# A gated linear attention and differential attention decoder on one core: runs of alternating half-array products, a bias table read from shifted copies, fewer zero products, another order in the router

## The chip, the cores and the metric

The kernel runs on one core of one Trainium2 chip. Its time is the device time of one execution in microseconds (us). The engines of the core work from queues of their own: TensorE (PE, with its weight loads PEld), VectorE (DVE), ScalarE (ACT), GpSimd (POOL) and SyncE (SP), which here issues nearly all transfers.

## What is computed

Two layers over 256 tokens of 1024 features, batch 1, all in float32. Layer 0 mixes the tokens with gated linear attention (four heads, a state of 128 x 256 for each, carried over four chunks of 64 tokens), layer 1 with differential attention (eight heads, two score maps of 64 features each, a bias from a table of relative positions). After each mixer stand a layer norm, a mixture of 16 experts with a hierarchical router (best group of four, then the two best experts in it), and another layer norm.

```python
def step(state, inp):                       # gated linear attention, per chunk of 64 tokens
    q_c, k_c, v_c, dec = inp
    state = dec[..., None] * state + jnp.einsum('bhck,bhcv->bhkv', k_c, v_c)
    o = jnp.einsum('bhck,bhkv->bhcv', q_c, state)
    return state, o

bias = rel_table[rel_bucket(kpos[None, :] - qpos[:, None])].transpose(2, 0, 1)
def probs(qb, kk):                          # differential attention
    s = jnp.einsum('bhqd,bhkd->bhqk', qb, kk) * scale + bias
    return jax.nn.softmax(jnp.where(visible, s, NEG_INF), axis=-1)
w = probs(q1b, k1) - lam * probs(q2b, k2)

for e in range(16):                         # mixture of experts
    hdn = jax.nn.silu(t @ w_gate[e]) * (t @ w_up[e])
    y = y + combine[:, e:e + 1] * (hdn @ w_down[e])
```

## The kernel before

**Order.** The code is written as a list of operations on tiles; a planner orders each engine's queue from it by the order of the text, by modelled costs and by when buffers are free, and `tc.issue_after(x)` puts an operation behind x in the queue of its engine. So operations of later lines can stand ahead of earlier ones that still wait, as long as no such rule forbids it.

**Weights.** SP loads all weights into a ring of 16 slots of 1 MB (`ring_slot`, L246; `load_cols`, L249; `load_moe`, L266) and three spare tiles x0 to x2 (`spare_tile`, L290). A slot is filled again when its last reader is done. The first 16 tiles of the first mixture go into the ring while the first mixer runs; `late_loads` (L338) queues the others, the table for the attention's bias and the weights of layer 1.

**The recurrence** (`head_proj`, L926; `head_scan`, L957). For each of four heads a projection of 8 steps runs on TensorE, with the weights split in two halves by ACT (L118) and DVE (L119). `head_scan` then goes chunk pair by chunk pair: two products k^T v (L964), which read the upper and the lower 64 rows and write two PSUM banks (`pB`, of which there are two), then for each of the two chunks a DVE step that decays the state and adds the product (L969, L971), and a product with the queries (L973), which writes the upper or lower half of the output partitions. The scan of one head is written after the projection of the next.

**The bias table.** `constants` (L358) makes a table of 8 heads x 384 positions and writes it to DRAM (`tvd`, L387, on POOL's queue). `late_loads` reads it back as T1 with each partition one element further on (L342). Partition p needs the window that starts at 127 - p, so T1 is upside down; `flip` (L1018) turns it with four products with a reversal matrix (L1023) and four ACT copies (L1024) into T, and POOL writes the mask (L1025). `moe` calls it as `side` behind expert 9 of the first mixture (L808).

**The router** (`out_norm`, L424; `norm_rstd`, L223; the head of `moe`, L464). The logits are taken from the tokens before the layer norm, gathered in `pl`, copied by DVE (L448) and folded by a product (L452); the mean and the reciprocal deviation then correct them (L457, L460). DVE compares them (L490 to L499), TensorE counts positions (L503, L504) and DVE makes one-hot matrices (L516). Meanwhile ACT applies the layer norm to the tokens in four pieces (L479), with the bias `nr` of L475, and splits them (L529); the gather products (L548) need both.

**The mixtures.** For each expert: 16 products with gate and up weights (L604), 8 with the down weights (L632), transposes (L589, L620) and a scatter (L664). The last one is `down_last` (L644).

**Between the mixtures' end and the attention** TensorE runs 25 zero products (`zero`, L179, its record is L181; called at L818) while DVE and ACT do the second layer norm (L837 to L843). Then `transposes` (L167) turns the tokens, with nine more zero products (`filler=9`, L1046) between the first and the second block of tokens of its first pair, and `affine_T` (L1034) scales and splits the result on ACT and DVE.

**The scores** (L1058). For each pair of heads, for each head, for each block of 128 queries: two products of 64 rows (L1071), one for each map, into one bank; DVE adds the bias and takes the minimum (L1073), ACT the exponential (L1076).

Of the kernel before, what the change touches and what calls it, by code (L numbers as in the profile page):

```python
# [10 lines left out]
F32 = mybir.dt.float32  # L11
# [32 lines left out]
def body(ctx, tc, x, w_in, wa_out, kv_w, wq, wb_out, wg, wu, wd, gate2, rows, rtab, lng, lnb, cblob, pblob, onehot, out):  # L44
# [25 lines left out]
    def sm(shape, tag, dt=F32, bufs=2):  # L70
        return small.tile(shape, dt, tag=tag, bufs=bufs, name=nm(tag))
# [150 lines left out]

    def norm_rstd(st, nd):  # L223
        a = sm([128, 2], "lna")
        dve.tensor_mul(a, nd, nd)
        dve.tensor_scalar(a, a, -EPS, None, op0=ALU.add)
        v = sm([128, 2], "lnv")
        for b in range(2):
            dve.tensor_scalar(v[:, b:b + 1], st[1][:, b, 0:1], st[1][:, b, 1:2], 1.0 / D, op0=ALU.add, op1=ALU.mult)
        dve.tensor_sub(v, v, a)  # L230
        y = sm([128, 2], "lny")
        act.activation(y, v, AF.Abs_reciprocal_sqrt)
        newton(y, v, a)
        return y

# [54 lines left out]
    def spare_tile(i, shape, dt, name):  # L290
        return spare.tile(shape, dt, tag=f"x{i}", bufs=1, name=name)
# [42 lines left out]
    next(moe_loads)  # L334
    tvd = dram.tile([8, 384], F32, name="tvd")
    late = {}

    def late_loads():  # L338
        moe_loads.send([spare_tile(j, [128, 2048], F32, nm("W")) for j in (2, 0, 1)])
        T1 = spare_tile(1, [128, 8, 256], F32, "T1")  # L340
        tap = tvd[:]
        sp.dma_start(T1, bass.AP(tensor=tap.tensor, offset=tap.offset, ap=[[1, 128], [384, 8], [1, 256]]))  # L342
        next(moe_loads)
        late["T1"] = T1
        late["v"] = [load_cols([(kv_w, 1024, 512)])]
        late["p"] = [load_cols([(wq[0], h * 128, 128), (wq[0], 512 + h * 128, 128), (kv_w, h * 128, 128), (kv_w, 512 + h * 128, 128)]) for h in range(4)]
        late["v"].append(load_cols([(kv_w, 1536, 512)]))
        late["o"] = [load_cols([(wb_out[0], j * 512, 512)]) for j in range(2)]
        late["m"] = load_moe(1, M1)
        next(late["m"])  # L350
# [7 lines left out]
    def constants():  # L358
# [27 lines left out]
        dve.tensor_scalar(tv, p[0:8, 0:384], -1.0, None, op0=ALU.mult)  # L386
        pool.dma_start(tvd, tv)  # L387

        lp = scr[0:1, 1792:1920].rearrange("p (q f) -> p q f", q=2)
# [34 lines left out]
    def out_norm(mp, layer, slots, xs, scale, xtf):  # L424
# [22 lines left out]
        lt = mp.tile([128, S], F32, tag="hi", bufs=3, name=nm("lt"))  # L447
        dve.tensor_copy(lt, pl[:, 0:256])  # L448
        rstd = norm_rstd(st, nd)
        pl = pB()  # L450
# [7 lines left out]
        for b in range(2):  # L458
            bs = slice(b * 20, b * 20 + 20)
            dve.scalar_tensor_tensor(lgf[:, bs], lgf[:, bs], rstd[:, b:b + 1], rowb[layer][:, 1], op0=ALU.mult, op1=ALU.add)  # L460
        return lg, rstd, nd, fold


    def moe(layer, M, lg, rstd, nd, fold, side=None):  # L464
        with tc.tile_pool(name=f"moe{layer}", bufs=1) as mp:
# [7 lines left out]

            nr = sm([128, 2], "nr")
            dve.tensor_mul(nr, nd, rstd)  # L475
            for h in range(2):
# [339 lines left out]
            if layer == 0:  # L816
                p = pB()
                for i in range(25):  # L818
                    zero(p)
# [106 lines left out]
    def head_proj(h, side=iter(())):  # L926
# [28 lines left out]
        return qT, kd, v  # L955

    def head_scan(h, qT, kd, v):  # L957
        st = None
        po = pC()
        for b in range(2):  # L960
            pk = [pB(), pB()]
            for cc in range(2):
                rs = slice(cc * 64, cc * 64 + 64)
                pe.matmul(pk[cc][:, 0:256], kd[rs, b], v[rs, b], start=True, stop=True)  # L964
            for cc in range(2):
                c = 2 * b + cc
                ns = scr[:, c % 3 * 256:c % 3 * 256 + 256]
                if c == 0:
                    dve.tensor_copy(ns, pk[cc][:, 0:256])  # L969
                else:  # L970
                    dve.scalar_tensor_tensor(ns, st, dec[:, h, c:c + 1], pk[cc][:, 0:256], op0=ALU.mult, op1=ALU.add)  # L971
                st = ns
                pe.matmul(po[cc * 64:cc * 64 + 64, b * 256:b * 256 + 256], qT[:, c * 64:c * 64 + 64], ns, start=True, stop=True)  # L973
        act.activation(o_sb[:, :, h * 256:h * 256 + 256], po.rearrange("p (b d) -> p b d", b=2), AF.Copy)
# [42 lines left out]

    def flip():  # L1018
        T1 = late["T1"]
        late["T"] = T = spare_tile(0, [128, 8, 256], F32, "T")  # L1020
        for q in range(4):
            p = pC()
            pe.matmul(p, cb[:, C_AN:C_AN + 128], T1[:, 2 * q:2 * q + 2].rearrange("p h j -> p (h j)"), start=True, stop=True)  # L1023
            act.activation(T[:, 2 * q:2 * q + 2].rearrange("p h j -> p (h j)"), p, AF.Copy)  # L1024
        pool.memset(T[0:64, :, 192:256], 1e30)  # L1025

    moe(0, M0, *rt_, flip)


    with tc.tile_pool(name="mix1", bufs=1) as mp:  # L1030
# [3 lines left out]
        def affine_T(kp, p):  # L1034
# [10 lines left out]
            dve.tensor_sub(xlo[:, 2 * kp:2 * kp + 2], f, xhi[:, 2 * kp:2 * kp + 2])  # L1045
        transposes(xa, affine_T, filler=9)  # L1046
        xs = lambda k: (xhi[:, k], xlo[:, k])
# [10 lines left out]
        def scores(hp, qk):  # L1058

            res = []  # L1060
            for hh in range(2):
                h = 2 * hp + hh
                rs = slice(hh * 64, hh * 64 + 64)
                wt_ = wx[:, h % 4]
                for b in range(2):
                    n = 128 * (b + 1)
                    p = pB()
                    sc = mp.tile([128, 2, 256], F32, tag="sc", bufs=2, name=nm("sc"))
                    m_ = sm([128, 2], "mrow", bufs=4)
                    for w in range(2):  # L1070
                        pe.matmul(p[:, w * 256:w * 256 + n], qk[rs, w, b * 128:b * 128 + 128], qk[rs, 2 + w, 0:n], start=True, stop=True)  # L1071
                    for w in range(2):
                        dve.tensor_tensor_reduce(out=sc[:, w, 0:n], in0=p[:, w * 256:w * 256 + n], in1=T[:, h, 256 - n:256], scale=1.0, scalar=3e38,  # L1073
                                                 op0=ALU.add, op1=ALU.min, accum_out=m_[:, w:w + 1])
                    for w in range(2):
                        act.activation(sc[:, w, 0:n], sc[:, w, 0:n], AF.Exp, scale=-1.0, bias=m_[:, w:w + 1], accum_out=es[:, b, h, w:w + 1])  # L1076
# [5 lines left out]
                res.append(wt_)  # L1082
            return res

# [124 lines left out]
```

## Time and profile before

| | before |
|---|---|
| median of 3 runs | 780.58 us (780.30 to 781.99) |
| the profiled execution | 782.23 us, of which the span is 780.6 us |
| PE, PEld | 751.2 us (96%), 404.2 us (52%) |
| DVE, ACT, POOL | 362.7 us (46%), 299.7 us (38%), 8.4 us (1%) |
| HBM | 244.19 MB read, 1.06 MB written, 315 GB/s in the mean |
| mean granted TensorE clock | 0.991 |

The span is the time from the first to the last instruction of the program; the rest of the time lies around it. Matmuls are pipelined and their ends are modelled, so a busy PE says that the matmul queue has work, not how much of the array is used. A float32 product appears as two records. An engine name with q is its sequencer; "issue" is time in which an engine waited for nothing that the profile shows. In a row, "out<-in" names the tiles that are written and read.

### The profile page before, as it was taken

The page shows a single profiled execution, that of the slowest core. Times are in us where ns is not written, and L with a number is a line of the kernel's source. Part 1 is how long each engine was busy: PE and PEld are TensorE (multiplying, and loading weights), DVE is VectorE, ACT ScalarE, POOL GpSimd, SP SyncE. Part 2 cuts the span into 40 slices and gives each one's busy share as a digit, 9 for nine tenths or more (in the row PEclk, how much of TensorE's full clock was granted, in tenths as well). Part 3 has the DMA queues.
Part 4 walks back from the last instruction along what each step waited for, and adds up shares of the span by engine and source line. Part 5 has one row for each costly group of instructions (what it writes and reads, how often), then busy time and mean ns, then how long its engine had stood idle before and what let it go on. Part 6 is the DMA issues. An engine that isn't in the chain of part 4 may idle for free. (4 is left out here: it accounts for less than half of the span.)

```text
span 780.6 us, 10650 instructions
## 1 busy us (share of the span) xinstructions
PE 751.2 (96%) x3762; PEld 404.2 (52%) x3762; DVE 362.7 (46%) x959; ACT 299.7 (38%) x655; POOL 8.4 (1%) x20
## 2 busy tenths in 40 slices
PE   7999999999999999999899999999999999999993
PEld 5887677534333433433689887763343243343331
DVE  3645576533363422422567777773344432332225
ACT  4444466523222331312557666562132232242123
POOL 1100000000000000000000000000000000000000
PEclk9999999999999999999999999999999999999997
DMA  7999448499999999999998336619999999999941
GB/s 217 312 385 392 168 164 295 152 381 397 394 386 393 392 395 396 393 392 367 290 363 314 144 111 215 216 56 370 393 395 395 394 391 390 397 394 392 391 168 56
DMA packets 131792, 246.02 MB, mean 315 GB/s; under 512 B 7916, under 2 KB 38101, under 8 KB 131734
## 3 DMA queue, kind: packets, MB, share of 16 engines
q1 hardware_dynamic: 131270, 244.68, 86.3%
q8 instruction: 32, 0.52, 0.3%
q10 hardware_dynamic: 432, 0.59, 0.2%
q14 instruction: 26, 0.21, 0.1%
q0 software_dynamic: 32, 0.01, 0.0%
HBM read 244.19 MB, written 1.06 MB: 314 GB/s over the span
## 5 line engine op out<-in xcount | busy, mean ns | idle before, releaser
L604 PE MATMUL pB<-W,xg 128*64 128x512 f32 x1056 | 258.7, 602 | 0.0
L604 PEld LDWEIGHTS pB<-W,xg 128*64 128x64 f32 x1056 | 69.1, 136 | 117.1 <-issue 110.2
L632 PE MATMUL pC<-W,ht 128*64 128x512 f32 x248 | 112.9, 594 | 0.0
L632 PE MATMUL pB<-W,ht 128*64 128x512 f32 x248 | 112.9, 594 | 0.0
L640 ACT ACTIVATE o<-pB,wst 64x512 fp32r<-64x512 f32 x31 | 21.1, 682 | 221.8 <-PE pC L632 208.4
L591 DVE TENSOR_SCALAR st<-pC 128x256 fp32r<-128x256 f32 x33 | 14.0, 425 | 155.2 <-PE pC L589 155.2
L119 DVE TENSOR_TENSOR lo<-W,hi 128x512 fp32r<-128x512 f32 x96 | 66.3, 696 | 39.9 <-PE pA L128 26.4
L118 ACT ACTIVATE hi<-W 128x512 fp32r<-128x512 f32 x96 | 59.5, 630 | 51.4 <-PE pA L129 29.8
L632 PEld LDWEIGHTS pB<-W,ht 128*64 128x64 f32 x248 | 33.3, 137 | 62.8 <-issue 61.2
L664 PE MATMUL pA<-o,st 128*128 128x512 f32 x132 | 40.2, 423 | 2.7 <-DVE o L658 2.1
L623 DVE COPY ht<-pC 128x256 f32<-128x256 f32 x33 | 14.0, 424 | 60.8 <-PE pC L620 60.7
L613 DVE TENSOR_TENSOR hd<-sl,pB 128x256 f32<-128x256 f32 x33 | 13.9, 422 | 56.7 <-ACT sl L611 56.6
L548 PE MATMUL pC<-OH,xs 128*128 128x256 f32 (+1 forms) x256 | 36.4, 292 | 3.1 <-ACT xg L555 1.9
L664 PEld LDWEIGHTS pA<-o,st 128*128 128x128 f32 x132 | 21.9, 188 | 33.5 <-issue 23.5
L548 PEld LDWEIGHTS pC<-OH,xs 128*128 128x128 f32 x256 | 32.8, 190 | 10.9 <-ACT xs L529 6.1
L127 PE MATMUL pA<-x1Thi,hi 128*128 128x256 f32 x128 | 36.5, 288 | 0.0
L632 PEld LDWEIGHTS pC<-W,ht 128*64 128x64 f32 x248 | 33.3, 137 | 6.1 <-issue 5.1
L128 PE MATMUL pA<-x1Tlo,hi 128*128 128x256 f32 x128 | 36.2, 285 | 0.0
L129 PE MATMUL pA<-x1Thi,lo 128*128 128x256 f32 x128 | 35.6, 288 | 0.0
L611 ACT ACTIVATE sl<-pB 128x256 f32<-128x256 f32 x33 | 12.7, 385 | 58.6 <-PE pB L604 58.4
L128 PE MATMUL pA<-lo,xThi 128*128 128x384 f32 (+1 forms) x96 | 35.0, 364 | 0.0
L129 PE MATMUL pA<-hi,xTlo 128*128 128x384 f32 (+1 forms) x96 | 34.7, 361 | 0.0
(340 smaller groups left out, 1148.1 us busy)
## 6 DMA issues: line engine op xcount, KB each, us to landing
W<-in_moe_w_gate_dram SPq DMA_DIRECT2D x132, 512.0 KB, 10.9
W<-in_moe_w_up_dram SPq DMA_DIRECT2D x132, 512.0 KB, 10.8
W<-in_moe_w_down_dram SPq DMA_DIRECT2D x66, 1024.0 KB, 12.0
W<-in_a_w_in_dram SPq DMA_DIRECT2D x16, 256.0 KB, 6.3
W<-in_a_w_in_dram SPq DMA_DIRECT2D x4, 1024.0 KB, 13.3
W<-in_a_w_out_dram SPq DMA_DIRECT2D x4, 1024.0 KB, 14.9
W<-in_kv_w_dram SPq DMA_DIRECT2D x4, 1024.0 KB, 8.9
W<-in_b_w_q_dram SPq DMA_DIRECT2D x16, 256.0 KB, 5.4
```

The source lines that it names most:

```text
L118: act.activation(hi, src, AF.Copy)
L119: dve.tensor_sub(lo, src, hi)
L127: pe.matmul(o, l[0], r[0], start=first, stop=False, skip_group_check=skip)
L128: pe.matmul(o, l[0], r[1], start=False, stop=False, skip_group_check=skip)
L129: pe.matmul(o, l[1], r[0], start=False, stop=last, skip_group_check=skip)
L548: pe.matmul(o, xs[k][:, q // 2, q % 2], OH[g][:, q % 2].rearrange("p e s -> p (e s)"), start=q == 0, stop=q == 3)
L591: dve.tensor_scalar(st, p[0:2 * m, 0:256], 0.0, None, op0=ALU.is_gt)
L604: mm = pe.matmul(p[c * m:c * m + m, 0:2 * fw].rearrange("p (g f) -> p g f", g=2), xg(k), w[:, :, kk, c * fw:c * fw + fw], start=k == 0, st ...
L623: dve.tensor_copy(ht, pt[:, 0:n * 128].rearrange("p (c t) -> p c t", c=n))
L632: mm = pe.matmul(p[2 * c // nt][c * m:c * m + m, 0:w], ht[:, q % n, (q // n) * m:(q // n) * m + m], wd_[q // 2][:, q % 2, c * w:c * w + w] ...
L640: act.activation(hi, src, AF.Copy, scale=ws[a:a + m, 0:1])
L664: pe.matmul(y[b][c], st[:, b * 128:b * 128 + 128], o[c], start=False, stop=last, skip_group_check=True)
```

## The change

Four parts. (1) `head_scan` issues the four products k^T v of a head as one run, with the lower and the upper rows in turn, then the four DVE steps with a place of its own for each state, then the four products with the queries as one run, from the last chunk to the first. `scores` takes the block of queries as the outer loop and issues the four products of both heads as one run, again in turn. `together` chains the products of a run by `issue_after`. (2) The table is written 128 times, one copy for each partition, to a second DRAM tile by a further transfer on POOL's queue; T is read from it directly, each partition from its own copy and one element earlier than the one before; the reversal products and the copies go, the mask stays. T takes x0 at the load, T1's x1 is not used. (3) 23 zero products in place of 25 after the first mixture, none in place of nine in the transposes. (4) `nr` is made in `norm_rstd`, and the copy of the logits is put behind it.

```diff
-    def norm_rstd(st, nd):
+    def norm_rstd(st, nd, nr):
         a = sm([128, 2], "lna")
...
         newton(y, v, a)
-        return y
+        return y, dve.tensor_mul(nr, nd, y)
...
+    tve = dram.tile([128, 8, 384], F32, name="tve")
...
-        T1 = spare_tile(1, [128, 8, 256], F32, "T1")
-        tap = tvd[:]
-        sp.dma_start(T1, bass.AP(tensor=tap.tensor, offset=tap.offset, ap=[[1, 128], [384, 8], [1, 256]]))
+        T = spare_tile(0, [128, 8, 256], F32, "T")
+        tap = tve[:]
+        sp.dma_start(T, bass.AP(tensor=tap.tensor, offset=tap.offset + 127, ap=[[8 * 384 - 1, 128], [384, 8], [1, 256]]))
         next(moe_loads)
...
         pool.dma_start(tvd, tv)
+        pool.dma_start(tve, tvd[:].unsqueeze(0).broadcast_to([128, 8, 384]))
...
-        dve.tensor_copy(lt, pl[:, 0:256])
-        rstd = norm_rstd(st, nd)
+        nr = sm([128, 2], "nr")
+        rstd, root = norm_rstd(st, nd, nr)
+        with tc.issue_after(getattr(root, "ins", root)):
+            dve.tensor_copy(lt, pl[:, 0:256])
...
-            nr = sm([128, 2], "nr")
-            dve.tensor_mul(nr, nd, rstd)
...
-                for i in range(25):
+                for i in range(23):
                     zero(p)
...
+    def together(mms):
+        prev = None
+        for mm in mms:
+            with tc.issue_after(prev) if prev else contextlib.nullcontext():
+                prev = mm()
+                prev = getattr(prev, "ins", prev)
+
     def head_scan(h, qT, kd, v):
-        st = None
+        pk = [pB(), pB()]
+        half = lambda cc: slice(cc * 64, cc * 64 + 64)
+        col = lambda b: slice(b * 256, b * 256 + 256)
+        together([lambda b=b, cc=cc: pe.matmul(pk[cc][:, col(b)], kd[half(cc), b], v[half(cc), b], start=True, stop=True) for b in range(2) for cc in (1, 0)])
+        st = []
+        for c in range(4):
+            ns, p = scr[:, c * 256:c * 256 + 256], pk[c % 2][:, col(c // 2)]
+            if c == 0:
+                dve.tensor_copy(ns, p)
+            else:
+                dve.scalar_tensor_tensor(ns, st[-1], dec[:, h, c:c + 1], p, op0=ALU.mult, op1=ALU.add)
+            st.append(ns)
         po = pC()
-        for b in range(2):
-            pk = [pB(), pB()]
-            for cc in range(2):
-                rs = slice(cc * 64, cc * 64 + 64)
-                pe.matmul(pk[cc][:, 0:256], kd[rs, b], v[rs, b], start=True, stop=True)
-            for cc in range(2):
...
-                pe.matmul(po[cc * 64:cc * 64 + 64, b * 256:b * 256 + 256], qT[:, c * 64:c * 64 + 64], ns, start=True, stop=True)
+        together([lambda c=c: pe.matmul(po[half(c % 2), col(c // 2)], qT[:, c * 64:c * 64 + 64], st[c], start=True, stop=True) for c in (3, 2, 1, 0)])
...
-    def flip():
...
-    moe(0, M0, *rt_, flip)
+    def mask():
+        pool.memset(late["T"][0:64, :, 192:256], 1e30)
+
+    moe(0, M0, *rt_, mask)
...
-        transposes(xa, affine_T, filler=9)
+        transposes(xa, affine_T)
...
         def scores(hp, qk):
-            for hh in range(2):
-                h = 2 * hp + hh
-                for b in range(2):
-                    n = 128 * (b + 1)
-                    p = pB()
...
-                    for w in range(2):
-                        pe.matmul(p[:, w * 256:w * 256 + n], qk[rs, w, b * 128:b * 128 + 128], qk[rs, 2 + w, 0:n], start=True, stop=True)
+            hs = (2 * hp, 2 * hp + 1)
+            for b in range(2):
+                n = 128 * (b + 1)
+                ps = [pB(), pB()]
+                rows_ = lambda hh: slice(hh * 64, hh * 64 + 64)
+                together([lambda w=w, hh=hh: pe.matmul(ps[hh][:, w * 256:w * 256 + n], qk[rows_(hh), w, b * 128:b * 128 + 128], qk[rows_(hh), 2 + w, 0:n], start=True, stop=True)
+                          for w in range(2) for hh in (1, 0)])
+                for h, p in zip(hs, ps):
```

## Rows read from the trace of the kernel before

**Rows 1.** Stages: length; PE, PEld, DVE, ACT, POOL busy (xcount); clock; DMA share; GB/s.
```profile
30.00:92.00 62.00, 61.85 (x316) 47.58 (x315) 31.53 (x65) 27.58 (x60) 1.43 (x2) 0.97 0.93 327
...
149.00:365.00 216.00, 214.53 (x966) 80.18 (x964) 74.16 (x176) 55.17 (x119) 0.52 (x1) 1.00 1.03 388
376.00:392.00 16.00, 13.89 (x66) 10.88 (x67) 10.94 (x24) 10.08 (x20) 0.31 (x2) 1.00 1.15 291
392.00:480.00 88.00, 87.83 (x593) 77.32 (x592) 64.00 (x218) 55.49 (x143) 0.00 (x0) 1.00 0.65 229
```

**Rows 2.** Matmul queue's waits, 10:765, first row: total us, times, longest.
```profile
PE pC L548 <- ACT xg L555: 1.9, 4, 0.6
```

**Rows 3.** SP in order of time: start us, us, engine, line.
```profile
39.96 11.43 SPq L259 DMA_DIRECT2D W<-in_a_w_out_dram  x4
...
218.87 0.41 SPq L342 DMA_DIRECT2D T<-tvd  x1
...
348.14 1.74 SPq L286 DMA_DIRECT2D W<-in_moe_w_down_dram  x2
```

**Rows 4.** Transfer issues, from the page: count, KB each, us to landing.
```profile
W<-in_moe_w_down_dram SPq DMA_DIRECT2D x66, 1024.0 KB, 12.0
```

**Rows 5.** PE in order of time, first mixture's end: [idle before <-releaser].
```profile
371.89 0.43 PE L652 MATMUL pB<-W,ht 128*64 128x256 f32 x1 [0.52 <-DVE ht L623]
```

**Rows 6.** PE in order of time, recurrence: start us, us, xcount of records merged.
```profile
45.66 0.65 PE L973 MATMUL pC<-scr,hq 128*64 128x256 f32 x4
46.24 0.70 PE L964 MATMUL pB<-hq 64*128 64x256 f32 x4
...
77.40 0.70 PE L964 MATMUL pB<-hq 64*128 64x256 f32 x2
```

**Rows 7.** PE by line, 30:92: xcount | busy us, mean ns | idle.
```profile
L973 PE MATMUL pC<-scr,hq 128*64 128x256 f32 x32 | 9.5, 404 | 0.2
L964 PE MATMUL pB<-hq 64*128 64x256 f32 x32 | 8.3, 435 | 0.0
```

**Rows 8.** PE in order of time, scores of the first pair of heads.
```profile
416.66 1.13 PE L1071 MATMUL pB<-qk 64*128 64x256 f32 x4
```

**Rows 9.** PE groups by line, 405 to 480 us.
```profile
L1071 PE MATMUL pB<-qk 64*128 64x128 f32 (+1 forms) x64 | 12.4, 346 | 0.2
```

**Rows 10.** PE in order of time, the reversal products in the first mixture.
```profile
287.00 3.69 PE L1023 MATMUL pC<-T,cb 128*128 128x512 f32 x8
```

**Rows 11.** POOL in order of time, 25 to 300 us.
```profile
31.71 0.72 POOL L387 DMA_DIRECT2D tvd<-scr  x1 [1.00 <-DVE scr L386]
291.39 0.52 POOL L1025 MEMSET T<- 64x512 f32 x1 [258.97 <-ACT T L1024]
```

**Rows 12.** PE in order of time, before the attention.
```profile
383.95 0.38 PE L174 MATMUL pC<-ident_r,xa 128*128 128x128 f32 x2
384.09 2.21 PE L181 MATMUL pB<-zero_r 128*128 128x512 f32 x9
```

**Rows 13.** ACT in order of time, the same place.
```profile
382.97 1.45 ACT L843 ACTIVATE xa<-pA,nr,rstd 128x512 f32<-128x512 f32 x2 [0.99 <-DVE nr L840]
386.56 1.02 ACT L1040 ACTIVATE x1Thi<-pC,pb 128x256 fp32r<-128x256 f32 x2 [2.14 <-PE pC L174]
```

**Rows 14.** ACT in order of time, router of layer 0.
```profile
138.95 2.92 ACT L479 ACTIVATE xa<-xa,nr,lny 128x512 f32<-128x512 f32 x4 [2.49 <-DVE nr L475]
```

**Rows 15.** DVE in order of time, router of layer 0.
```profile
137.03 0.42 DVE L448 COPY lt<-pB 128x256 f32<-128x256 f32 x1 [0.37 <-PE pB L445]
...
141.14 0.76 DVE L516 TENSOR_TENSOR OH<-posm,cb 128x256 fp32r<-128x256 f32 x2
```

**Rows 16.** PE in order of time, router of layer 0.
```profile
142.24 2.39 PE L548 MATMUL pC<-OH,xs 128*128 128x256 f32 x16 [0.60 <-ACT xs L529]
```

**Rows 17.** Two neighbouring stretches of the recurrence stage, columns as before.
```profile
33.00:36.40 3.40, 3.40 (x12) 2.94 (x11) 2.20 (x5) 0.63 (x1) 0.00 (x0) 0.50 1.14 319
36.40:40.00 3.60, 3.60 (x24) 3.60 (x24) 1.38 (x2) 1.27 (x2) 0.00 (x0) 1.00 1.12 333
```

More of the change, by code (lines that the diff above doesn't have):

```diff
@@ L339, in late_loads @@
         moe_loads.send([spare_tile(j, [128, 2048], F32, nm("W")) for j in (2, 0, 1)])
-        T1 = spare_tile(1, [128, 8, 256], F32, "T1")
-        tap = tvd[:]
-        sp.dma_start(T1, bass.AP(tensor=tap.tensor, offset=tap.offset, ap=[[1, 128], [384, 8], [1, 256]]))
+        T = spare_tile(0, [128, 8, 256], F32, "T")
+        tap = tve[:]
+        sp.dma_start(T, bass.AP(tensor=tap.tensor, offset=tap.offset + 127, ap=[[8 * 384 - 1, 128], [384, 8], [1, 256]]))
         next(moe_loads)
-        late["T1"] = T1
+        late["T"] = T
         late["v"] = [load_cols([(kv_w, 1024, 512)])]
@@ L460, in out_norm, with moe @@
             dve.scalar_tensor_tensor(lgf[:, bs], lgf[:, bs], rstd[:, b:b + 1], rowb[layer][:, 1], op0=ALU.mult, op1=ALU.add)
-        return lg, rstd, nd, fold
-    def moe(layer, M, lg, rstd, nd, fold, side=None):
+        return lg, rstd, nr, fold
+    def moe(layer, M, lg, rstd, nr, fold, side=None):
         with tc.tile_pool(name=f"moe{layer}", bufs=1) as mp:
@@ L955, in head_proj @@
         return qT, kd, v
-    def head_scan(h, qT, kd, v):
-        st = None
-        po = pC()
-        for b in range(2):
-            pk = [pB(), pB()]
-            for cc in range(2):
-                rs = slice(cc * 64, cc * 64 + 64)
-                pe.matmul(pk[cc][:, 0:256], kd[rs, b], v[rs, b], start=True, stop=True)
-            for cc in range(2):
[L966 to L972, printed above, removed]
-                pe.matmul(po[cc * 64:cc * 64 + 64, b * 256:b * 256 + 256], qT[:, c * 64:c * 64 + 64], ns, start=True, stop=True)
+    def together(mms):
[4 more added lines that the diff above has]
+                prev = getattr(prev, "ins", prev)
+    def head_scan(h, qT, kd, v):
+        pk = [pB(), pB()]
[10 more added lines that the diff above has]
+            st.append(ns)
+        po = pC()
+        together([lambda c=c: pe.matmul(po[half(c % 2), col(c // 2)], qT[:, c * 64:c * 64 + 64], st[c], start=True, stop=True) for c in (3, 2, 1, 0)])
         act.activation(o_sb[:, :, h * 256:h * 256 + 256], po.rearrange("p (b d) -> p b d", b=2), AF.Copy)
@@ L1016, in body @@
     mix0.__exit__(None, None, None)
-    def flip():
[L1019 to L1025, printed above, removed]
-    moe(0, M0, *rt_, flip)
+    def mask():
+        pool.memset(late["T"][0:64, :, 192:256], 1e30)
+    moe(0, M0, *rt_, mask)
     with tc.tile_pool(name="mix1", bufs=1) as mp:
@@ L1058, in scores @@
         def scores(hp, qk):
-            res = []
-            for hh in range(2):
-                h = 2 * hp + hh
-                rs = slice(hh * 64, hh * 64 + 64)
-                wt_ = wx[:, h % 4]
-                for b in range(2):
-                    n = 128 * (b + 1)
-                    p = pB()
+            hs = (2 * hp, 2 * hp + 1)
[6 more added lines that the diff above has]
+                for h, p in zip(hs, ps):
+                    wt_ = wx[:, h % 4]
                     sc = mp.tile([128, 2, 256], F32, tag="sc", bufs=2, name=nm("sc"))
                     m_ = sm([128, 2], "mrow", bufs=4)
-                    for w in range(2):
-                        pe.matmul(p[:, w * 256:w * 256 + n], qk[rs, w, b * 128:b * 128 + 128], qk[rs, 2 + w, 0:n], start=True, stop=True)
                     for w in range(2):
@@ L1081, in scores @@
                     dve.scalar_tensor_tensor(wv, sc[:, 1, 0:n], c_[:, 0:1], sc[:, 0, 0:n], op0=ALU.mult, op1=ALU.add)
-                res.append(wt_)
-            return res
+            return [wx[:, h % 4] for h in hs]
         def pv_T(ws, tile_):
```

## The prediction

> **What bounds the kernel now.** I read the stage table first, then the waits, then the order of time of single engines. In the stage table [rows 1] the column to look at is PE against the stretch's length: 61.85 of 62 us in the recurrence stage, 214.53 of 216 in the first mixture, 87.83 of 88 in the attention stage, at a granted clock of 0.97 to 1.00. A busy TensorE is not yet a TensorE that sets the pace, since a matmul's end is modelled; so I looked at the waits. The largest that the matmul queue shows after the start-up is 1.9 us in four pieces [rows 2], it is for an activation, and no weight transfer is among the matmul queue's waits. TensorE's issue order is therefore the path almost from end to end, and what is taken off it shortens the kernel, provided the weights still come in time.
>
> That proviso is the second thing to read. The DMA share is 1.03 in the first mixture [rows 1], so the transfers have no room there and can't be pulled forward by a faster TensorE. But they run ahead: the last two down tiles of layer 0 are issued at 348.14 [rows 3], land in about 12.0 us [rows 4], thus by some 362, and the first product that reads them starts at 371.89 [rows 5]. That is 10 us in hand at the worst place. In the recurrence and the attention stage the share is 0.93 and 0.65 [rows 1]: the ring is full for a part of each, so an earlier mixture frees its slots earlier and the whole stream moves with it.
>
> **The recurrence.** A float32 product of 64 rows is two passes on TensorE, and a pass is one record. The row of 46.24 shows four records of L964 in 0.70 us, the row of 77.40 two records in the same 0.70 [rows 6]: two products on opposite halves of the rows take the time of one. The row of 45.66 shows the same for L973 on opposite halves of the output partitions. The old order mostly misses this: all 32 products of both lines are 8.3 + 9.5 = 17.8 us of busy TensorE [rows 7], that is 0.56 each, as if nearly all stood alone. After the change each head is one run of four L964-type products and one run of four L973-type products. What two pairs in a run cost isn't shown; the nearest row is the 1.13 us of four records of 256 columns in the scores [rows 8], which are two products in a row without a switch between; two pairs are the same number of passes, if the halves run side by side. The other end is that a run of four is worked off in series, without switches: eight passes, which by the spacing inside that same row ((1.13 - 0.70) / 2 = 0.22 more for each pass beyond two) is 0.70 + 6 x 0.22 = 2.0 us. So eight runs cost 8 x 1.13 = 9.0 us or 8 x 2.0 = 16 us: a gain of 8.8 or of 1.8. I take the first, as the pairs of [rows 6] did run side by side. The new order adds a wait: the first of the second run needs the state after all four DVE steps, and behind it in TensorE's queue stand the next projection's products. For heads 0 to 2 the planner can lay the next projection between the runs; for head 3 there are only the first products of the gate projection, whose split halves come through the same DVE. Its own DVE chain is four steps, which the old order also needed. I charge 1.3 us for such waits (between 0 and 1.9 us a head: four DVE steps at the stage's mean, 31.53 / 65 = 0.49 [rows 1]): the recurrence gives **-7.5 us**.
>
> **The scores.** The 32 products of L1071 are 12.4 us of TensorE [rows 9]. After it each pair of heads has two runs: four products of 128 columns, of 128 and four of 256. The second is again two pairs of 256 columns, 1.13 us [rows 8]; the first has half the columns, and by the same spacing (0.11 a pass) some 0.75. Four pairs of heads cost 4 x 1.9 = 7.5 us: **-4.8 us**, and nothing (12.4 against 4 x 3.2 = 12.7) if the halves don't overlap. Each run now holds both score banks until DVE has read both heads; the second run waits for that. The cover is the next projection; where it is gone (the last pair of heads) the value projection stands behind. DVE is busy 64.0 of 88 us there [rows 1], so I charge nothing more.
>
> **The flip.** The four products with the reversal matrix are 8 records, 3.69 us, in the middle of the first mixture [rows 10], back to back with the expert products; they, and four ACT copies, go. Since TensorE is the path there and the weights have 10 us in hand, all of it counts: **-3.6 us**. The price is the table's write: one transfer on POOL's queue that repeats 12 KB 128 times in DRAM. The small write before it costs POOL 0.72 us for 8 rows [rows 11]; 1024 rows can cost as little, or 128 times as much (92 us). POOL has nothing else until the mask, as the 258.97 us of idle in front of that show, and SP reads the copies at 218.87 [rows 3]; either end is covered. The 1.6 MB are about 5 us of transfers at the stage's 327 GB/s [rows 1]; behind them in time are the last weights of this stage, issued from 39.96 on [rows 3], which are used only after both gate projections. Bounds 0 and +5, nearest to 0: I take 0. The read itself has the same number of bytes and runs as before and the same place in SP's queue.
>
> **The fillers.** After the first mixture 25 zero products end and the first transposes follow at 383.95; then nine more zero products hold the transposes' second half back for 2.21 us [rows 12]. What they cost is read on ACT: its normalisation ends at 384.42, and the next thing it does, the first affine step, starts at 386.56 after 2.14 us of waiting for a transpose [rows 13]. Without the nine it would wait some 0.3 us, and with two zero products fewer ahead of it nothing: **-2.1 us**. What comes late next is this affine step itself, on ACT and DVE, as now.
>
> Against this edit speaks a rule of the Trainium skill. What the row shows: the granted clock stays 1.00 in the whole transition from 376 to 392 us [rows 1], transposes and waits among it. The Trainium skill's page "TensorE: Matmul & The Clock Gate", section "Part 4: PE-mode transpose", says that transposes don't count as TensorE activity for the clock as products do; by that rule the stretch without the nine fillers would let the clock fall to 1.2 GHz, and the sum would be 1.7 us worse.
>
> **The router** (twice). The bias of the normalisation, nr, is made after the logits now; ACT waits 2.49 us for it and then normalises from 138.95 [rows 14]. In the new order nr comes before the copy of the logits, some 1.6 us earlier; the copy of 137.03 [rows 15] slips by one short DVE step, some 0.2 us. The first gather product starts at 142.24 after 0.60 us of waiting for ACT's split [rows 16]; the one-hot matrices were ready at 141.90 [rows 15]. So the other input allows only 0.3 us at the start; but ACT's later work in the gather, a table load among it, also moves up and TensorE stalls less in its second half. Bounds +0.2 (the copy's slip alone) and -0.9, middle -0.6 for each layer: **-1.2 us**.
>
> **The sum.** 7.5 + 4.8 + 3.6 + 2.1 + 1.2 = 19.2 us. The profiled execution has a span of 780.6 and a time of 782.23 us; the median of the runs shown is 780.58, so the profiled one lies 0.2% above it. Span and what lies around it move alike: 782.2 - 19.2 = 763.0 on the profiled execution's scale, and 780.6 - 19.2 = **761.4 us** on that of the median.
>
> **The rivals.**
> 1. The halves don't overlap in longer runs. For it: no row shows a run of two pairs. Against: both kinds of pair in [rows 6]. The recurrence gives 1.8, the scores nothing: 1.8 + 3.6 + 2.1 + 1.2 = 8.7, hence 772.
> 2. The clock falls behind the shortened fillers. How dear that is, the stretch from 33.0 to 36.4 shows: at a granted clock of 0.50 it holds 12 matmuls, the next 3.6 us at 1.00 hold 24 [rows 17]; one such stretch costs 1.7 us: 763. Against: the transition's clock of 1.00 so far, with waits in it. The Trainium skill's rule above speaks for it.
> 3. The weights become the bound in the first mixture. If the 10 us in hand are an error of my reading (a landing is a median), flip, fillers and router give nothing until the attention stage: 7.5 + 4.8 = 12.3, hence 768.
> 4. Slower: the runs, each kept together, stand at the head of TensorE's queue and wait. Its place is the first product of each of the 16 runs. A head's first run can wait for three copies of its projection (at ACT's mean of 27.58 / 60 = 0.46, 1.4 us), its second for the four DVE steps (1.9), a score run for four reductions to leave the banks (at DVE's mean of 64.00 / 218 = 0.29, 1.2 us) [rows 1], and nothing behind can pass. At the full price that is 4 x 3.3 + 8 x 1.2 = 22.8 us in place of the 1.3 charged: 783. The point from which it decides is a mean wait of 20.5 / 16 = 1.3 us a run. Against: TensorE has a projection's products to lay between.
> 5. It doesn't do what it says: were the pairs put apart by other products, it would be rival 1's time or a little more.
>
> **How the numbers follow.** My forecast 0.62; rival 1 with 5, 0.12; rival 2, 0.17; rival 3, 0.05; rival 4, 0.04. The least time is all the better ends: 8.8 + 4.8 + 3.6 + 2.1 + 1.8 = 21.1, and 1.7 more if the slow stretch at 33 us is gone: 758; with the modelled ends of the scores' runs (some 0.1 us a run) about 756. Upwards the range reaches into rival 3 and to the edge of rival 1: 770. Both sides of the range are left out with about 0.2. Measurements of this kernel can't tell less than about 0.2% from no change. Faster 0.95, same 0.01, slower 0.04.
>
> **What would show it.** In the profile after: the recurrence's lines with about 9 to 10 us of TensorE and the scores' with about 7.5, in eight runs each; L1023's group gone; ACT's wait before the first affine step under 0.3 us; ACT's wait for nr about 1 us, not 2.49; and a stretch of clock 0.50 only near 33 us. The sum is wrong if the matmul queue shows waits for the state or for the score banks of more than some 0.3 us a run, if a weight transfer appears among its waits, or if a second stretch of 0.50 appears.

## The result, and the profile after

The changed kernel takes **772.38 us** (median of 4, 771.65 to 773.84), the kernel before 780.86 in the same session (780.30 to 781.99): a ratio of 0.9892, 95% interval 0.9872 to 0.9912, or 8.5 us less. 761.4 had been forecast, and 770 was the upper end of the range.

The profiled execution has a span of 770.0 us, 10.6 less than that of before. 1.4 to 1.5 us of this difference are not the change: the stretch of clock 0.50 near 33 us, which the profile before had [rows 17], is missing in this one. The timed executions of the changed kernel fall into groups 0.9 to 1.2 us apart that go with their mean clock (0.995, 0.991, 0.989), so one such stretch comes in some executions and not in others; the last section returns to it.

Following the same piece of work through both traces gives the ledger. The shift is that of the first product or transpose behind each stage; a minus is time gained:

| stage | forecast | shift gained in it | how it ends |
|---|---|---|---|
| recurrence | -7.5 | -8.7, of it 1.4 the missing slow stretch | first transpose of the gated output 98.09 to 89.34 |
| router and mixture 0, up to the reversal | -0.6 | **+2.2** | -6.6 after the third gather |
| reversal of the table | -3.6 | -3.5 | -10.1 at the end of the first mixture |
| fillers | -2.1 | -2.1 | -12.2 at the first query and key projection |
| scores and attention | -4.8 | **0.0** | -12.25 at the transposes of the attention's output (482.63 to 470.38) |
| router and mixture 1 | -0.6 | **+1.8** | -10.5 behind its first two experts, and to the end |

So three of the steps came as forecast, and two didn't: the router lost 4.0 us where it should have gained 1.2, and the scores gained nothing. The stages of the changed kernel, with the columns of [rows 1]:

```profile
30.00:84.00 54.00, 54.00 (x321) 45.44 (x322) 31.09 (x60) 27.86 (x61) 2.01 (x3) 1.00 1.05 376
140.00:356.00 216.00, 215.12 (x966) 79.98 (x964) 73.60 (x172) 53.00 (x117) 0.52 (x1) 1.00 1.02 384
366.00:380.00 14.00, 11.86 (x56) 8.89 (x57) 10.95 (x24) 10.20 (x20) 0.31 (x2) 1.00 1.13 289
380.00:470.00 90.00, 87.14 (x610) 76.61 (x609) 64.49 (x219) 55.96 (x150) 0.00 (x0) 1.00 0.71 250
```

The last row is the one to look at: in the attention stage TensorE was busy in 87.83 of 88 us before, and now stands still for 2.9 of 90. (The two stretches don't hold quite the same work; for that the ledger is there.) The transition keeps a clock of 1.00 without the nine fillers.

**What went right.** The recurrence by line, and two runs of it in order of time:

```profile
L973 PE MATMUL pB<-hq 64*128 64x256 f32 x32 | 5.9, 412 | 0.0
L983 PE MATMUL pC<-scr,hq 128*64 128x256 f32 x32 | 4.3, 392 | 0.0
57.55 1.13 PE L973 MATMUL pB<-hq 64*128 64x256 f32 x8
61.66 1.08 PE L983 MATMUL pC<-scr,hq 128*64 128x256 f32 x8
```

L973 is now k^T v, which was L964 with 8.3 us, and L983 the product with the queries, which was L973 with 9.5 us [rows 7]. A whole run of four products (eight records) takes the 1.1 us that the forecast took. Measured without modelled ends (from the start of the product ahead of a run to the start of the one behind it, less one step of the former), both lines cost 18.2 us before and 10.4 now. The transition, TensorE and then ACT:

```profile
368.32 5.26 PE L181 MATMUL pB<-zero_r 128*128 128x512 f32 x23 [0.53 <-ACT warm L823]
373.71 1.06 PE L174 MATMUL pC<-ident_r,xa 128*128 128x128 f32 x8
...
372.88 1.45 ACT L846 ACTIVATE xa<-pA,nr,rstd 128x512 f32<-128x512 f32 x2 [0.99 <-DVE nr L843]
374.38 1.02 ACT L1044 ACTIVATE x1Thi<-pC,pb 128x256 fp32r<-128x256 f32 x2
```

The first eight of the sixteen transposes now stand in one piece, and the first affine step follows the normalisation without a wait, where it waited 2.14 us in [rows 13].

**What went wrong in the router.** ACT, VectorE and TensorE of layer 0 in order of time:

```profile
128.55 2.93 ACT L482 ACTIVATE xa<-xa,nr,lny 128x512 f32<-128x512 f32 x4 [0.82 <-DVE nr L234]
...
132.54 0.43 DVE L519 TENSOR_TENSOR OH<-posm,cb 128x256 fp32r<-128x256 f32 x1
132.88 1.43 DVE L533 TENSOR_TENSOR xs<-xa,xs 128x256 fp32r<-128x256 f32 x4
134.22 0.42 DVE L519 TENSOR_TENSOR OH<-posm,cb 128x256 fp32r<-128x256 f32 x1
...
133.06 0.48 PE L551 MATMUL pC<-OH,xs 128*128 128x256 f32 x2
134.69 0.62 PE L551 MATMUL pC<-OH,xs 128*128 128x256 f32 x3 [1.15 <-DVE OH L519]
```

ACT's wait for nr fell from 2.49 [rows 14] to 0.82, as forecast. But with ACT early, its split x is early too, and four low-half splits of 1.43 us are now ready while VectorE makes the first one-hot matrix. They take the place between the two one-hots, which stood together in [rows 15]. Each group of four gather products needs both, so TensorE issues two products and waits 1.15 us.

A second loss comes at the first expert's down products. TensorE again:

```profile
148.12 1.88 PE L607 MATMUL pB<-W,xg 128*64 128x512 f32 x6
149.94 0.44 PE L623 MATMUL pC<-ident_r,hd 128*128 128x128 f32 x2
150.30 1.50 PE L607 MATMUL pB<-W,xg 128*64 128x512 f32 x5
151.22 0.59 PE L635 MATMUL pB<-W,ht 128*64 128x512 f32 x1
151.64 0.59 PE L607 MATMUL pB<-W,xg 128*64 128x512 f32 x1
151.65 0.59 PE L635 MATMUL pB<-W,ht 128*64 128x512 f32 x1
...
154.65 1.02 PE L635 MATMUL pC<-W,ht 128*64 128x512 f32 x2
```

An expert product fills half of the array (128x64) and runs beside its neighbour on the other half: one pair of records each 0.43 us, two such steps a pair of products. Such a product is two records, and I call it a half product. Here the transposes of L623 stand behind an odd number of half products. The one ahead of them runs alone (the last two of the six records, 0.43 us apart), the pairs behind are made of unlike neighbours (L607 with L635), and the last down product is left alone too: 0.85 us. Counted through the trace, 60 records of L607 and L635 have no partner within 0.1 us, 48 in the kernel before.

**What went wrong in the scores.** The group, then the waits of the matmul queue and the largest of the weight loads' (380 to 470 us; total us, times, longest):

```profile
L1069 PE MATMUL pB<-qk 64*128 64x128 f32 (+1 forms) x64 | 8.4, 354 | 0.5 <-ACT qk L1127 0.5
PE pA L129 <- DVE lo L119: 1.3, 3, 0.7
PE pB L1069 <- ACT qk L1127: 0.5, 1, 0.5
PE pA L128 <- DVE lo L119: 0.5, 1, 0.5
PE pC L1091 <- DVE crow L1082: 0.2, 1, 0.2
PEld pA L129 <- DVE lo L119: 2.6, 5, 0.9
```

The runs are shorter (8.4 against 12.4 us in [rows 9]; by the distance to the next product 9.4 against 13.2). But TensorE now waits in six places, 3.6 us by the same measure, mostly for lo: the low half of a weight split for the *next* projection. One of the six, 0.7 us, stands in a score run, waits for ACT's copy of qk and is in the 9.4 already; three more places cost under 0.3 us each. The largest place, VectorE and TensorE:

```profile
407.40 0.42 DVE L1076 CUSTOM_DVE_ANT_0 sc<-pB,T 128x256 f32<-128x256 f32 x1
...
408.01 0.68 DVE L419 SCALAR_TENSOR_TENSOR xa<-pC,xa 128x512 f32<-128x512 f32 x1
...
408.62 0.42 DVE L1076 CUSTOM_DVE_ANT_0 sc<-pB,T 128x256 f32<-128x256 f32 x1
...
409.18 0.41 DVE L1076 CUSTOM_DVE_ANT_0 sc<-pB,T 128x256 f32<-128x256 f32 x1
...
409.64 0.69 DVE L119 TENSOR_TENSOR lo<-W,hi 128x512 fp32r<-128x512 f32 x1
...
410.38 0.39 PE L129 MATMUL pA<-x1Thi,lo 128*128 128x256 f32 x1 [0.68 <-DVE lo L119]
```

Both heads' scores arrive together, so VectorE has the reductions and followers of two heads in one heap, without a gap from 406.9 on; the split of L119 comes behind them, and there are only two buffers of low halves to bridge that.

### The profile page after: what moved, and what is told of

It is laid out like the page before. It is cut to its first block, busy times and chain, and to the rows that moved or that the text cites. A ratio compares the mean times of both kernels' runs of the same rounds, so it can differ in the third digit from the quotient of the medians.

```text
span 770.0 us, 10596 instructions
## 1 busy us (share of the span) xinstructions
PE 737.5 (96%) x3743; PEld 397.0 (52%) x3743; DVE 362.3 (47%) x959; ACT 297.2 (39%) x651; POOL 8.9 (1%) x21
## 5 line engine op out<-in xcount | busy, mean ns | idle before, releaser
L607 PE MATMUL pB<-W,xg 128*64 128x512 f32 x1056 | 261.4, 602 | 0.2
L607 PEld LDWEIGHTS pB<-W,xg 128*64 128x64 f32 x1056 | 69.8, 136 | 118.2 <-issue 111.5
L635 PE MATMUL pB<-W,ht 128*64 128x512 f32 x248 | 112.9, 594 | 0.0
L635 PE MATMUL pC<-W,ht 128*64 128x512 f32 x248 | 112.9, 594 | 0.0
L119 DVE TENSOR_TENSOR lo<-W,hi 128x512 fp32r<-128x512 f32 x96 | 66.5, 696 | 37.4 <-PE pA L128 25.2
L635 PEld LDWEIGHTS pB<-W,ht 128*64 128x64 f32 x248 | 33.3, 137 | 62.0 <-issue 59.8
L635 PEld LDWEIGHTS pC<-W,ht 128*64 128x64 f32 x248 | 33.3, 137 | 7.0 <-issue 6.3
L127 PE MATMUL pA<-hi,xThi 128*128 128x384 f32 (+1 forms) x96 | 34.6, 366 | 0.0
## 6 DMA issues: line engine op xcount, KB each, us to landing
W<-in_moe_w_up_dram SPq DMA_DIRECT2D x132, 512.0 KB, 10.8
```

What stands on the lines that cost most here:

```text
L119: dve.tensor_sub(lo, src, hi)
L127: pe.matmul(o, l[0], r[0], start=first, stop=False, skip_group_check=skip)
L607: mm = pe.matmul(p[c * m:c * m + m, 0:2 * fw].rearrange("p (g f) -> p g f", g=2), xg(k), w[:, :, kk, c * fw:c * fw + fw], start=k == 0, st ...
L635: mm = pe.matmul(p[2 * c // nt][c * m:c * m + m, 0:w], ht[:, q % n, (q // n) * m:(q // n) * m + m], wd_[q // 2][:, q % 2, c * w:c * w + w] ...
```

## The experiments

Each run is timed against the kernel before in the same session (780.9 to 781.8 us there); differences below are from the changed kernel's 772.38 unless another run is named.

**1. The old scores.** `scores` as before, all else changed.

> The changed kernel with the old scores alone (head by head, two products in a row). Theory A, that the paired score runs save 3.8 us of TensorE (13.2 down to 9.4 by the distance to the next product) and that 3.6 us of it come back as waits of the projection's third products for the low halves of split weights: the time stays at 772.4, within 1 us, the score runs cost 13 us again, and the waits for the low halves go. Rival B, that the scores gave the 4.8 us of the forecast and something else lost them: 777.2.

772.39 us (ratio 0.9889, 0.9875 to 0.9903): no difference. The trace has the 12.4 us of score products back, not one wait in the matmul queue of this stage, and the stage ends within 0.4 us of the same place. Theory A holds: what the runs save comes back as waits.

**2. The old router.** nr, the copy of the logits and their order as before.

```diff
-        rstd, root = norm_rstd(st, nd, nr)
-        with tc.issue_after(getattr(root, "ins", root)):
-            dve.tensor_copy(lt, pl[:, 0:256])
+        dve.tensor_copy(lt, pl[:, 0:256])
+        rstd = norm_rstd(st, nd)
...
+            nr = sm([128, 2], "nr")
+            dve.tensor_mul(nr, nd, rstd)
```

> The changed kernel with the old order in the router alone (nr after the logits). Theory A, that the new order puts low-half splits between the two one-hot matrices, which costs 0.8 us in each layer before the first expert product, and shifts a transpose between the two halves of an expert product, which costs another 0.85: 3.3 us less than the changed kernel, 769.1. Rival B, that the new order gained its 0.6 us a layer and the loss comes from elsewhere in the mixture: 773.6, and the two lone half products stay.

767.68 us (ratio 0.9829, 0.9817 to 0.9842): 4.7 less, more than A's 3.3. In the trace 4.0 us are gained, 2.15 in layer 0 and 1.8 in layer 1: at the first expert product 0.9, at the first down products 0.85, and in layer 0 another 0.4 at the third gather, where the changed kernel has four records alone that this one hasn't. This is the changed kernel's largest loss, and the step of the router alone made it.

**3. The old recurrence.** `head_scan` as before.

> The changed kernel with the old recurrence alone. Theory A, that runs of two pairs work side by side (18.2 us of TensorE before, 10.4 after, by the distance to the next product): 7.8 us more, 780.2. Rival B, that the halves don't overlap in longer runs and the total came to 772 for that reason: 1.8 us more, 774.2. Rival C, that 1.3 of the shift of 8.7 us in the profile was the half-speed stretch near 33 us that this one profile lacks: 7.4 more, 779.8, which only differs from A in the profile.

780.09 us (ratio 0.9988, 0.9979 to 0.9996): 7.7 more. Its profile has no slow stretch at 33 us either, and from the first product of the recurrence to the transposes behind it takes 7.4 us longer. B falls: the halves do run side by side. C is right for the profile: 1.3 to 1.5 of the 8.7 us in the ledger were the stretch.

**4. Both one-hots first.** The low-half splits of the first gather held behind them.

```diff
-            xs0 = [split_x(k, dve) for k in range(4)]
+            hot = one_hot(0)
+            xs0 = [split_x(k, dve, None, hot) for k in range(4)]
...
-                eng.tensor_sub(t[:, 1], x_, t[:, 0])
+                with after(hot):
+                    eng.tensor_sub(t[:, 1], x_, t[:, 0])
```

> The changed kernel with the low-half splits of the first gather held behind both one-hot matrices of it. Theory A: the 1.15 us of waiting for the second one-hot in each layer go, and the first gather product starts some 0.5 us earlier than in the kernel before relative to the fold, so 0.8 to 1.3 us a layer, 770 to 770.8; the transpose between two halves of an expert product can stay, and if it does the two lone half products (0.85 us a layer) stay too. Rival B, that the gather then waits for the low halves instead, since these come later: no change, 772.4.

769.23 us (ratio 0.9851, 0.9837 to 0.9866): 3.15 less. In the trace the first expert product comes 1.4 us earlier in each layer, but TensorE lays the second half of the gather in two pieces between expert products and 0.35 us are gone again at the first down product: 1.05 us a layer stay, inside A's 0.8 to 1.3. The records that run alone stay (60). B falls. The median is 1 us lower than these 2.1 us explain, less than one slow stretch.

**5. Both one-hots first, and an even place for the transposes.**

```diff
                 mm = gu_part(M[e][0], (0,), xg, p, 2)
+                if e == 1:
+                    mm = gu_part(M[e][0], (1,), xg, p, 2, (0,))
                 if prev is not None:
                     with tc.issue_after(getattr(mm, "ins", mm)):
                         ht = tr_part(prev[0], 2)
-                mm = gu_part(M[e][0], (1,), xg, p, 2)
+                mm = gu_part(M[e][0], (1,), xg, p, 2, (1,) if e == 1 else (0, 1))
```

> The kernel with both one-hot matrices first, and in addition the transposes of expert 0 held behind the sixth half-width product of expert 1, an even place, where the planner had put them behind the fifth. Theory A, that each cut between the two halves of an expert product leaves two products that run alone, 0.43 us each: 0.85 us less in each layer than with the one-hots alone, 769.2 - 1.7 = 767.5, and the lone records near the first down products go. Rival B, that the lone records cost nothing because TensorE waits for something else there: 769.2.

767.85 us (ratio 0.9836, 0.9822 to 0.9849): 1.4 less than run 4, 1.75 by the traces. VectorE, then TensorE, of this run; to compare with the rows of the changed kernel:

```profile
132.64 0.76 DVE L519 TENSOR_TENSOR OH<-posm,cb 128x256 fp32r<-128x256 f32 x2
133.32 1.43 DVE L534 TENSOR_TENSOR xs<-xa,xs 128x256 fp32r<-128x256 f32 x4
...
133.17 2.32 PE L552 MATMUL pC<-OH,xs 128*128 128x256 f32 x16
...
147.58 1.46 PE L608 MATMUL pB<-W,xg 128*64 128x512 f32 x6
148.97 0.44 PE L624 MATMUL pC<-ident_r,hd 128*128 128x128 f32 x2
149.34 1.08 PE L608 MATMUL pB<-W,xg 128*64 128x512 f32 x4
```

Sixteen gather products without a wait, and six records of half products in 1.46 us where the changed kernel took 1.88. So the new order of the router, with these two side effects gone, is level with the old one (767.85 and 767.68 in run 2). It is 0.5 us ahead at layer 0's first expert product, and 0.1 us at the first down product; the four lone records at the third gather, which stay, take 0.4. The 1.2 us of the forecast don't appear in either form.

**6 and 7. The second half of the softmax later.** It is written into the next projection, behind its splits 2 and 4, or 3 and 5.

```diff
+            if k in (2, 4):
+                next(side2, None)
...
+            soft(1, hs[0], ps[0])
+            yield
+            soft(1, hs[1], ps[1])
+            yield
```

> The changed kernel with the softmax of the second query block of each pair of heads written later, into the next projection behind its splits 2 and 4, so that the low-half splits of the weights stand ahead of it on VectorE. Theory A, that the 3.6 us of waiting in the attention stage come from the order on VectorE (four reductions and their followers ahead of a split): most of it goes, 769 to 771. Rival B, that VectorE and ScalarE are full there and the wait only moves: 772.4.

> As the run with splits 2 and 4, but behind splits 3 and 5. Theory A, order on VectorE: 769 to 771, the more the later the softmax stands. Rival B, load and not order: 772.4; and if the score banks are then read too late for the next pair of heads, the wait moves to the score runs: 772.4 or more.

769.78 us (ratio 0.9855, 0.9840 to 0.9870) and 770.60 (0.9864, 0.9849 to 0.9879): 2.6 and 1.8 less. The same products, reductions and splits, in another order. In run 6 the stage is 2.95 us shorter, and these waits are left in the matmul queue:

```profile
PE pB L1074 <- ACT qk L1152: 0.5, 1, 0.5
PE pA L128 <- DVE lo L119: 0.5, 1, 0.5
PE pA L127 <- ACT og1Thi L197: 0.3, 1, 0.3
```

Order, not load: A. Its "the more the later" is wrong: behind 3 and 5 the stage gains 2.4 us only, since a second score run now waits (0.8 us ahead of the second pair of heads), and that profile has a slow stretch more (at 507 us).

**8. The fillers back.**

```diff
-                for i in range(23):
+                for i in range(25):
...
-        transposes(xa, affine_T)
+        transposes(xa, affine_T, filler=9)
```

> The changed kernel with the fillers of before (25 zero products at the end of the first mixture and nine among the transposes). Theory A, that the transition is a chain on TensorE and ScalarE and the fillers delayed it: 2.0 us more, 774.4, with a granted clock of 1.00 in the transition in both. Rival B, that without the fillers the clock falls after the transition: then this kernel shows a higher clock in 376 to 400 us than the changed one, and the same or less time.

775.66 us (ratio 0.9936, 0.9922 to 0.9949): 3.3 more. 1.95 of it is the delay; the rest is a stretch of half clock, and it stands in the kernel *with* the fillers. The same 3.5 us in the changed kernel and in this one, columns of [rows 1]:

```profile
369.00:372.50 3.50, 3.50 (x17) 3.06 (x17) 3.40 (x11) 1.31 (x3) 0.00 (x0) 1.00 1.15 293
```
```profile
369.00:372.50 3.50, 3.50 (x11) 2.77 (x10) 3.40 (x11) 1.32 (x3) 0.00 (x0) 0.54 1.11 290
```

B falls. The two programs are the same up to that point (0.02 us apart in their traces): both run zero products there, and the fillers that differ follow behind the stretch, so they can't have caused it. What did isn't settled.

**9. Half products kept together.** Run 5, and the first pair of a group's first expert laid between the two halves of its gather, pinned on both sides.

```diff
+                    if k == 4 and n == 4:
+                        pair = mid()
...
+                      with after(pair):
+                        gm = pe.matmul(o, xs[k][:, q // 2, q % 2], OH[g]
...
+                    with after(pinned[0]):
+                        mm = gu_part(M[e][0], (0,), xg, p, 2, (1,))
```

> The kernel of the run with even places, and in addition the first pair of half products of a group's first expert laid between the two halves of its gather, as a pair, with the rest behind the gather. In the planner's order 30 runs of expert products in the changed kernel have an odd number of half-width products (24 in the kernel before), here 14, and 26 in the run with even places. Theory A, that every product left without its other half costs 0.43 us wherever it stands: 12 fewer than with even places, 767.85 - 5.2 = 762.7. Rival B, that the lone products stand where TensorE would wait for the gather anyway: 767.85, and the saved time shows as waits of the gather.

763.54 us (ratio 0.9764, 0.9750 to 0.9777): 4.3 less than run 5, of A's 5.2; between executions of like mean clock (762.1 and 767.8) it is 5.7. The profile of run 9 has the stretch near 33 us and that of run 5 has not; from the first transpose of the gated output to the end, which lies behind it, run 9 is 5.2 us shorter. The records that run alone fall from 52 to 28, which is A's 12 products. A.

**10. Run 9 with the late softmax of run 6.**

> The run before this one, and the softmax of the second query block written later, behind splits 2 and 4 of the next projection. Theory A, that the two losses are independent: 2.6 us less than with the halves kept alone, 760.1 if that gives 762.7. Rival B, that another stage takes the time back: no less than with the halves kept.

**760.62 us** (ratio 0.9726, 0.9713 to 0.9740): 2.9 less than run 9. The losses are independent. This kernel is faster than the changed one, and by 21 us than the kernel before.

**11. The old router with the late softmax.**

> The changed kernel with the router of before and the late softmax, both measured alone (767.68 and 769.78). Theory A, independent: 772.4 - 4.7 - 2.6 = 765.1. Rival B: they share a cause, 767.7.

764.83 us (ratio 0.9790, 0.9776 to 0.9803): A's 765.1.

**12. The reversal back on TensorE.** `late_loads` and `flip` as before, no copies in DRAM.

> The changed kernel with the reversal of the bias table on TensorE as before, and without the shifted copies in DRAM. Theory A, that the four products lie on the path and the copies cost nothing: 3.5 us more, 775.9. Rival B, that the write of the 1.6 MB delayed weights somewhere and took a part of the gain: less than 2.5 us more.

776.67 us (ratio 0.9944, 0.9928 to 0.9960): 4.3 more, of which 3.5 appear in the trace across the reversal and 1.4 as a slow stretch in the transition of this one profile. B falls: the copies, 1536 KB that land in 10.5 us in the changed kernel and take 0.55 us of POOL, cost nothing that shows.

## Why the prediction was wrong

The forecast stood 11.0 us below the median. Two steps hold 10.0 of it.

**The router: forecast -1.2, measured +4.0 (ledger and trace of run 2; 4.7 by its time).** The step that failed is "Bounds +0.2 (the copy's slip alone) and -0.9". The upper bound counted what the moved instruction delays by standing in the way. It didn't count what the engine it sets free will trigger: an ACT that is 1.6 us earlier makes other work ready on VectorE, and the order there changes. The rows were at hand. Before, ACT's splits began after VectorE had started on the one-hots of [rows 15], and the four low-half splits stood just behind these, ACT first:

```profile
141.78 1.87 ACT L529 ACTIVATE xs<-xa 128x256 fp32r<-128x256 f32 x5
142.22 1.43 DVE L530 TENSOR_TENSOR xs<-xa,xs 128x256 fp32r<-128x256 f32 x4
```

An ACT that is 1.6 us earlier makes them ready ahead of the one-hots. The second part, half products left alone by an odd cut, was in the trace of before too (48 records) and was not looked for; since TensorE's queue there shows no wait, it doesn't appear in any table of waits.

**The scores: forecast -4.8, measured 0.0 (run 1).** Two errors. The term itself was 1.0 too large: 9.4 us of runs, not 7.5, against 13.2, not 12.4, because the attention's value products cut two of the eight and one of these waits 0.7 us. (Its 4.8 is also 12.4 less 7.6; with the 7.5 that it writes it would be 4.9.) And the step that failed is "DVE is busy 64.0 of 88 us there [rows 1], so I charge nothing more": it took an average share for an order. The busy time is the same after (64.49 of 90), yet 2.9 us were lost to work on VectorE that stood in the wrong place, 0.4 to 0.9 us at a time. The sign that the prediction named, waits for score banks, didn't come; the run's own wait for its copies came once (0.5 us). The price fell on the neighbour that shares VectorE.

**The recurrence: forecast -7.5, measured 7.7 by run 3 and 7.4 by its trace.** Right, also in its mechanism: 1.1 us a run. But the 1.3 us that it charged for waits fit by luck: no wait for the state appears, and what the runs cost above 9.0 (10.4 in all) is mostly two runs cut in two by other products.

**The reversal, the fillers, the copies: -3.6, -2.1 and 0, measured -3.5, -2.1 (1.95 by run 8's trace) and nothing.** Right. What remains of the 11.0 us, about 1, isn't resolved: it is less than one slow stretch, of which the executions hold different numbers.

**The rivals.** Rival 1 put 772, and the kernel took 772.4, but for another reason: its mechanism, halves that don't overlap, is refuted by runs 1 and 3 and by the 1.1 us rows. A total that fits is no evidence for the cause. Rival 2, the clock, didn't come in the changed kernel; the traces show 1.00 in the transition without the fillers and 0.54 with them in run 8. The rule of the Trainium skill ("TensorE: Matmul & The Clock Gate", "Part 4: PE-mode transpose") on transposes, by which the prediction let the clock fall without the fillers, isn't borne out by that 1.00. The stretch of run 8 ends at 372.2 us, ahead of the first transpose at 375.53, and says nothing on it. Rival 3 didn't come either: a single wait of the matmul queue is put down to a weight transfer, 0.3 us at a scatter, which reads no weights and waited as long before. Rival 4 had waits that the runs cause, but charged them to the runs; its 1.3 us a run came to 0.2 (3.6 us on 16 runs), and 2.9 of the 3.6 stood elsewhere. And of the signs that the prediction named most came (the recurrence's run lengths, the reversal's group, ACT's two waits, the clock; the scores' runs took 8.4 in place of 7.5 us): they were the signs of the steps that it had thought of, and none looked at VectorE's order.

## What to carry to other kernels

An instruction made earlier on one engine sets work free on the others, and a planner that takes what is ready will lay it in front of something more urgent: ask for each freed step what it now overtakes, and pin that. An engine at 70% can still be late for its neighbour when two heads' work arrives at once; read its order against the few buffers ahead of it, not its share. Where two products share the array, look at the distance of the records and not only at waits: 0.43 us for each one left without its other half shows in no table of waits, and keeping 12 more of them together brought 4.3 us here (run 9).

## What the runs showed of the hardware

The half-speed stretch (clock 0.50, the 1.2 GHz of the two levels) moves. In the profiles of these kernels it stands near 33 us (before, runs 6, 7, 9 and 10), near 369 or 372 us (runs 8 and 12), at 507 us (run 7, a second one) or nowhere ahead of the kernel's end, and costs 1.3 to 1.9 us where two traces show it. It doesn't go with an edit: run 8 has it in the same work that runs at 1.00 in the changed kernel. What it does go with near 33 us is the start. TensorE's first products run at half speed there (in the changed kernel 128x384 products take 320 ns to the next start at 9.79 us and 174 to 178 ns from 10.60 us on). In the five profiles with the stretch near 33 us the recorded clock of 1.00 begins between 8.3 and 9.1 us, in the nine others at 7.6 us (runs 3 and 4) or between 10.3 and 10.8 us. Why the two go together isn't shown, and no run changed that moment alone. A difference of 1.5 us between two profiles of such kernels should first be looked up in the clock column.

Two products on opposite halves of the array need not belong together: in the changed kernel L607 and L635, which belong to different experts, run side by side at 0.43 us a pair of records, like two halves of one expert. What counts in these traces is that they are neighbours on TensorE.
